# Where the sums of w_down for block 1 are made: in the second pass of block 0's second matrix, or in block 1's first matrix

## The chip, the core and the metric

The kernel runs on one core of a Trainium2 chip. The metric is the device time of one execution in microseconds; before the change it is 2035.29 us, the median of three runs (2033.35 to 2038.95). One execution was recorded by the hardware profiler. TensorE (PE) multiplies matrices, VectorE (DVE), ScalarE (ACT) and GpSimd (POOL) work on elements, SyncE (SP) issues DMA transfers. Each engine, and each queue of DMA issues, works in the order in which its instructions were written.

## The reference, cut to what matters

One layer: an S5 mixer with a gated linear unit, and behind it a gated feed-forward layer with a causal convolution of width 3, for 2048 frames, `D_MODEL` = 1024, `D_FF` = 2816. The change touches the feed-forward layer alone:

```python
def conv_ffn(xn, w_up, conv_w, conv_b, w_down):
    h = causal_dwconv(xn @ w_up, conv_w, conv_b)
    a, b = jnp.split(h, 2, axis=-1)
    return (jax.nn.silu(a) * b) @ w_down
```

`w_up` is 1024 x 5632 and `w_down` 2816 x 1024, in float32. The result is added to the residual.

## The kernel before

**Tiling.** The frames are taken in two blocks, `kb` = 0 and 1, of 1024 frames each. For each block the first matrix (`up`) multiplies by `w_up`, the convolution and the gate follow (`conv`), and the second matrix (`down`) multiplies by `w_down`. Float32 is kept by splitting each operand into a high and a low half in float16: one product is three matmuls of 128x512 (`mm3`, L76 to L78).

**First matrix.** It is done in 22 steps m, each by seven products in place of eight (a scheme of the Strassen kind over a 2x2 split). A product takes one weight chunk, a "unit" `("u", kb, m, i)`, and twelve matmuls into a PSUM bank `p`, of which six are in rotation. DVE and ACT take the banks out into `hu` (L1216 to L1230); the taps of the convolution (L1131, L1132) and the gate (L1135, L1137) follow some products later by a small calendar (`later`, `tick`).

**Second matrix.** Block 0 does it plainly, in two passes r = 0 and 1 over half of its frames each. A pass runs over 22 chunks f of 128 rows of `w_down`, two units `("p", 0, r, f, n)` each, with all eight PSUM banks `pq` in use, and starts on f = 0 and 1 together. Block 1 does it by seven products in four stages (`STAGES`), units `("d", 1, s, j, i)`. Five of the seven need sums or differences of rows j and j + 11 of `w_down`. With 11 values of j these are 55 sums; they are made ahead of time as units `("x", ...)` that no matmul uses, and are kept in DRAM.

**Weights.** `units` (L802 to L816) is the list of all units in the order in which they are fetched. `w_unit` (L876) takes the next of them, into the next of nine slots of a ring of `wc` tiles:

- If the chunk was made before, SyncE loads it from the DRAM tile `wcd`, 256 KB (L885).
- If not, it is made from float32 rows `fst` that SyncE has loaded, 512 KB each (L858, L861; four buffers). For a sum GpSimd first adds or subtracts (L907), into `xtmp` (one buffer) or in place. ACT then writes the high half (L908).
- At the next call of `w_units`, `w_flush` has DVE make the low half (L914), SyncE stores the chunk to `wcd` (L915), and rows used up are replaced by loads of the next ones.

`w_units` is called before each product with the index of that product's unit plus a lead: `LU` = 6 in the first matrix, `LD` = 5 in the second. The lead counts units, so those that no matmul uses count among them. At the end of each pass of block 0 the results are added to the residual tiles `res` (L1292) and stored; the 16 stores are issued by ACT (L1288). SyncE loads the residual (L1283).

Before the change the 55 sums stand in the second pass (r = 1) of block 0's second matrix, five per two f. Its own 44 units were made in the first pass and are read back from `wcd`. In block 1's first matrix all 154 units are read back from `wcd`.

Of the kernel before, what the change touches and what calls it, by code (L numbers as in the profile page):

```python
# [22 lines left out]
NF = 22  # L23
# [21 lines left out]
def tile_kernel(ctx: ExitStack, tc: tile.TileContext, x, meta, norm_mix, norm_ffn, w_in, lam_re, lam_im, log_dt,  # L45
# [95 lines left out]
    with ExitStack() as c2:  # L141
# [627 lines left out]
        p = NCB - 1  # L769
# [32 lines left out]
    units, loads, users = [], [], {}  # L802
    for kb_ in range(2):
        ms_ = range(2 * NP)
        seq_ = [(0, 1), (0, 2), (1, 1), (1, 2), (0, 4), (0, 7), (0, 5), (0, 6), (0, 3)] if kb_ == 0 else []
        for m in ms_:
            seq_ += [(m, i) for i in (1, 2, 6, 7, 4, 5, 3) if (m, i) not in seq_]
        units += [("u", kb_, m, i) for m, i in seq_]
        if kb_ == 0:
            sums = [("x", 0, s, j, i) for j in range(NH) for s, i in ((1, 0), (2, 0), (0, 0), (2, 1), (3, 0))]  # L810
            for r in range(2):
                for f in range(NF):
                    units += [("p", 0, r, f, 1), ("p", 0, r, f, 0)]
                    units += sums[len(sums) * f // NF:len(sums) * (f + 1) // NF] if r else []
        else:
            units += [("d", 1, s, j, i) for s, n in ((0, 2), (1, 2), (2, 2), (3, 1)) for j in range(NH) for i in range(n)]  # L816

# [636 lines left out]
```

## Time and profile before

| what | value |
|---|---|
| median of three runs | 2035.29 us |
| the profiled execution, its own time | 2040.73 us |
| its span, first to last instruction | 2038.9 us |
| mean granted TensorE clock | 0.979 |
| block 0, first matrix | about 758 to 1182 us of the span |
| block 0, second matrix, pass 0 / pass 1 | 1182 to 1301 / 1301 to 1430 us |
| block 1, first matrix / second matrix | 1430 to 1829 / 1829 to 2039 us |
| DMA moved | 329.92 MB, mean 162 GB/s |

How to read the rows that follow: a row of waits gives engine and line, what released it, the idle time in us in total, how often, and the longest. A row of the timeline gives start, duration, engine and line, what is written from what, and in brackets the idle time ahead of it with its releaser; a matmul's duration is longer than the step to the next one, since matmuls overlap. SPq and ACTq are the queues in which SyncE and ACT issue DMAs. Rows of the DMA view end in the median time from issue to landing. Rows of one line or tile give the durations in ns as min/median/max, or busy us and mean ns, then idle time and releasers.

### The profile page before, as it was taken

How to read it: one execution, taken by the hardware profiler on the slowest of the kernel's cores; microseconds unless marked ns; L12 is line 12 of the kernel's file. 1: busy time of each engine (PE TensorE's matmuls, PEld its weight loads, DVE VectorE, ACT ScalarE, POOL GpSimd, SP SyncE). 2: the span in 40 equal slices, each digit the busy share in tenths (PEclk: the TensorE clock that was granted, in tenths of full speed). 3: DMA queues.
4: the chain of work that ended last, by engine and by line, in shares of the span. 5: the costliest groups of instructions: out<-in, count | busy, mean ns of one | idle time of the engine just before them, and what ended most of it. 6: DMA issues, size and time to landing. Idle time of an engine off the chain costs nothing.

```text
span 2038.9 us, 28973 instructions
## 1 busy us (share of the span) xinstructions
PE 1923.3 (94%) x10992; PEld 957.5 (47%) x10992; DVE 1384.9 (68%) x1709; ACT 645.2 (32%) x1057; POOL 577.2 (28%) x644
## 2 busy tenths in 40 slices
PE   3699999689999999999999989999999999999999
PEld 3456666445444444444444434334444444444444
DVE  3489999944444348999999961345466666668982
ACT  5433423312222224544445441222222232322110
POOL 4221212400000014555555500366000001117630
PEclk9799999789999999999999999999999999999999
DMA  9967766958566656444444489999533333336443
GB/s 187 188 136 140 176 138 150 229 139 185 130 140 158 147 150 178 143 156 148 146 157 148 151 243 274 310 324 303 171 104 101 102 104 101 101 99 156 144 124 93
DMA packets 337223, 329.92 MB, mean 162 GB/s; under 512 B 150700, under 2 KB 238332, under 8 KB 337084
## 3 DMA queue, kind: packets, MB, share of 16 engines
q1 hardware_dynamic: 319164, 286.01, 52.9%
q0 software_dynamic: 8496, 27.30, 4.7%
q10 hardware_dynamic: 9424, 14.76, 2.9%
q8 instruction: 86, 1.41, 0.3%
q14 instruction: 53, 0.43, 0.1%
HBM read 183.82 MB, written 108.45 MB: 143 GB/s over the span
## 4 chain that ended last, share of the span: by engine, by line
PE 66%; DVE 8%; DMA 4%; issue 2%; ACT 1%; POOL 1%; SPq 1%; DVEq 0%; ACTq 0%; POOLq 0%
PE g L137 15%; PE p L78 11%; PE p L76 11%; PE p L77 11%; PE pq L76 3%; PE pq L77 3%; PE pq L78 3%; PE po L76 2%; PE po L77 2%; PE po L78 2%; DMA wc<-wcd 1%; DMA wcd<-wc 1%; DVE wc L914 1%; DVE y L1132 1%; DVE y L1131 1%
## 5 line engine op out<-in xcount | busy, mean ns | idle before, releaser
L76 PE MATMUL p<-hc,wc 128*128 128x512 f16 x1232 | 467.3, 379 | 2.3 <-DMA hc<-hl 1.7
L78 PE MATMUL p<-hc,wc 128*128 128x512 f16 x1232 | 467.5, 379 | 1.7 <-DVE wc L914 1.7
L77 PE MATMUL p<-hc,wc 128*128 128x512 f16 x1232 | 467.4, 379 | 0.9 <-DMA hc<-hl 0.9
L137 PE MATMUL g<-wg,yT 128*128 128x512 f16 x1536 | 334.3, 381 | 0.7 <-DMA yT<-yh 0.7
L914 DVE SCALAR_TENSOR_TENSOR wc<-fst,wc 128x512 f16<-128x512 f32 x209 | 184.7, 892 | 109.9 <-ACT wc L908 91.4
L137 PEld LDWEIGHTS <-yT 128*128 128x128 f16 x1536 | 150.2, 98 | 183.1 <-issue 2.6
L908 ACT ACTIVATE wc<-fst 128x512 f16<-128x512 f32 x209 | 125.9, 625 | 229.6 <-POOL fst L873 97.5
L78 PEld LDWEIGHTS <-wc 128*128 128x128 f16 x1232 | 120.2, 98 | 148.7 <-DVE wc L914 3.8
L76 PEld LDWEIGHTS <-wc 128*128 128x128 f16 x1232 | 120.1, 98 | 140.0 <-issue 1.8
L77 PEld LDWEIGHTS <-wc 128*128 128x128 f16 x1232 | 120.2, 98 | 138.9 <-DMA hc<-hl 1.2
L76 PE MATMUL pq<-wc,act 128*128 128x512 f16 x352 | 135.2, 384 | 16.6 <-DMA wc<-wcd 11.1
L76 PE MATMUL u<-hnT,win 128*128 128x512 f16 (+2 forms) x352 | 115.2, 337 | 25.6 <-DMA hnT<-hl 14.8
L77 PE MATMUL pq<-wc,act 128*128 128x512 f16 x352 | 135.1, 384 | 0.0
L78 PE MATMUL pq<-wc,act 128*128 128x512 f16 x352 | 134.8, 383 | 0.0
L77 PE MATMUL u<-hnT,win 128*128 128x512 f16 (+2 forms) x352 | 114.9, 337 | 16.9 <-DMA hnT<-hl 16.9
L76 PE MATMUL po<-wc,act 128*128 128x512 f16 x308 | 117.6, 382 | 3.4 <-DVE res L1292 3.4
L77 PE MATMUL po<-wc,act 128*128 128x512 f16 x308 | 117.6, 382 | 0.0
L78 PE MATMUL po<-wc,act 128*128 128x512 f16 x308 | 117.4, 381 | 0.0
L78 PE MATMUL u<-hnT,win 128*128 128x512 f16 (+2 forms) x352 | 115.0, 337 | 0.0
L1123 ACT ACTIVATE act<-hu,cwt 128x1024 f32<-128x1024 f32 x44 | 54.6, 1241 | 185.6 <-DVE hu L1224 141.3
L77 PEld LDWEIGHTS <-act 128*128 128x128 f16 x660 | 64.8, 98 | 99.1 <-issue 23.3
L1123 ACT ACTIVATE y<-hu,cwt 128x1024 f32<-128x1024 f32 x44 | 54.6, 1240 | 162.3 <-DVE hu L1224 123.2
(328 smaller groups left out, 2983.6 us busy)
## 6 DMA issues: line engine op xcount, KB each, us to landing
wc<-wcd SPq DMA_DIRECT2D x275, 256.0 KB, 2.7
wcd<-wc SPq DMA_DIRECT2D x253, 256.0 KB, 3.2
fst<-in_ffn_w_up_dram SPq DMA_DIRECT2D x44, 512.0 KB, 5.1
fst<-in_ffn_w_down_dram SPq DMA_DIRECT2D x44, 512.0 KB, 5.8
ud<-us SPq DMA_DIRECT2D x32, 258.0 KB, 5.3
U<-ud SPq DMA_DIRECT2D x16, 516.0 KB, 3.5
Toep<-kd SPq DMA_DIRECT2D x64, 128.0 KB, 5.4
yd<-yf POOLq DMA_DIRECT2D x8, 1024.0 KB, 7.6
```

What stands on the lines that cost most here:

```text
L76: PE.matmul(out=ps, lhsT=sh, rhs=mh, start=first, stop=False)
L77: PE.matmul(out=ps, lhsT=sh, rhs=ml, start=False, stop=False)
L78: PE.matmul(out=ps, lhsT=sl, rhs=mh, start=False, stop=last)
L137: PE.matmul(out=gps[t][o], lhsT=yT[t][:, a, dk], rhs=wg[b][:, dk, 512 * o:512 * o + 512], start=(dk == 0 and a + b == 0), stop=(dk == DK - ...
L908: A.activation(w[:, 0], src, AF.Copy, scale=GS)
L914: V.scalar_tensor_tensor(w[:, 1], src, GS, w[:, 0], op0=ALU.mult, op1=ALU.subtract)
L1123: A.activation(y, hu[:, 2:18], AF.Identity, bias=cwt[:, 3, c:c + 1], scale=cwt[:, 2, c:c + 1])
L1131: V.scalar_tensor_tensor(y, hu[:, 1:17], cwt[:, 1, c:c + 1], y, op0=ALU.mult, op1=ALU.add)
L1132: V.scalar_tensor_tensor(y, hu[:, 0:16], cwt[:, 0, c:c + 1], y, op0=ALU.mult, op1=ALU.add)
```

## The change

The 55 sums are taken out of the second pass and put between the units of block 1's first matrix: none in the first nine products, then two per five products, until the 143rd product of 154. Nothing else is edited; the number of instructions for the sums stays the same. All lines behind the edit have a number that is lower by one in the changed file (L915 is L914 there).

```diff
-        units += [("u", kb_, m, i) for m, i in seq_]
+        sums = [("x", 1, s, j, i) for j in range(NH) for s, i in ((1, 0), (2, 0), (0, 0), (2, 1), (3, 0))] * kb_
+        for n_, (m, i) in enumerate(seq_):
+            units.append(("u", kb_, m, i))
+            units += sums[max(0, n_ - 6) * 2 // 5:max(0, n_ - 5) * 2 // 5]
         if kb_ == 0:
-            sums = [("x", 0, s, j, i) for j in range(NH) for s, i in ((1, 0), (2, 0), (0, 0), (2, 1), (3, 0))]
-            for r in range(2):
-                for f in range(NF):
-                    units += [("p", 0, r, f, 1), ("p", 0, r, f, 0)]
-                    units += sums[len(sums) * f // NF:len(sums) * (f + 1) // NF] if r else []
+            units += [("p", 0, r, f, n_) for r in range(2) for f in range(NF) for n_ in (1, 0)]
```

**First place: SyncE's queue at the start of the second pass.** `wc<-wcd` loads a chunk of the pass (`wc_11611` is that of f = 0, `wc_11817` that of f = 3), `wcd<-wc` stores a chunk that was made. Before:

```order
L885 DMA wc_11611<-wcd 128x1024
L915 DMA wcd<-wc_11609 128x1024
L861 DMA fst_11639<-in_ffn_w_down_dram 128x1024
L885 DMA wc_11641<-wcd 128x1024
L915 DMA wcd<-wc_11643 128x1024
L885 DMA wc_11652<-wcd 128x1024
L915 DMA wcd<-wc_11649 128x1024
L885 DMA wc_11720<-wcd 128x1024
L915 DMA wcd<-wc_11722 128x1024
L885 DMA wc_11750<-wcd 128x1024
L885 DMA wc_11752<-wcd 128x1024
L915 DMA wcd<-wc_11744 128x1024
```

The same place in the changed kernel:

```order
L884 DMA wc_11611<-wcd 128x1024
L914 DMA wcd<-wc_11609 128x1024
L860 DMA fst_11639<-in_ffn_w_down_dram 128x1024
L884 DMA wc_11641<-wcd 128x1024
L884 DMA wc_11643<-wcd 128x1024
L884 DMA wc_11645<-wcd 128x1024
L884 DMA wc_11647<-wcd 128x1024
L884 DMA wc_11713<-wcd 128x1024
L884 DMA wc_11715<-wcd 128x1024
```

The stores of sums (all `wcd<-wc` behind the first) have left the queue, and loads of chunks follow each other.

**Second place: block 1's first matrix, early in its step m = 2.** SyncE's queue before is an unbroken row of chunk loads; in the changed kernel it reads:

```order
L914 DMA wcd<-wc_12653 128x1024
L860 DMA fst_12680<-in_ffn_w_down_dram 128x1024
L860 DMA fst_12682<-in_ffn_w_down_dram 128x1024
L884 DMA wc_12684<-wcd 128x1024
L884 DMA wc_12700<-wcd 128x1024
L914 DMA wcd<-wc_12702 128x1024
L884 DMA wc_12727<-wcd 128x1024
L884 DMA wc_12743<-wcd 128x1024
L884 DMA wc_12763<-wcd 128x1024
L914 DMA wcd<-wc_12765 128x1024
```

After each sum's store come two or three chunk loads; after the last sum of each j two loads of rows stand between. On DVE at the same place, before (`hu_2_1<-p_2_6` takes out the product i = 6 of m = 2, the rows on `y_1_1` are the taps and the gate of m = 1):

```order
L1220 TENSOR_TENSOR hu_2_1_12982<-p_2_6_13008,hu_2_1_12982 128x512
L1131 SCALAR_TENSOR_TENSOR y_1_1_12963<-hu_1_1_12853,cwt,y_1_1_12963 128x1024
L1132 SCALAR_TENSOR_TENSOR y_1_1_12963<-hu_1_1_12853,cwt,y_1_1_12963 128x1024
L1135 SCALAR_TENSOR_TENSOR y_1_1_12963<-act,y_1_1_12963 128x512
L1135 SCALAR_TENSOR_TENSOR act<-act,y_1_1_12963 128x512
L1222 TENSOR_TENSOR hu_2_1_12982<-p_2_7_13029,hu_2_1_12982 128x512
```

and in the changed kernel:

```order
L1219 TENSOR_TENSOR hu_2_1_12670<-p_2_6_12706,hu_2_1_12670 128x512
L1130 SCALAR_TENSOR_TENSOR y_1_1_12648<-hu_1_1_12527,cwt,y_1_1_12648 128x1024
L1131 SCALAR_TENSOR_TENSOR y_1_1_12648<-hu_1_1_12527,cwt,y_1_1_12648 128x1024
L1134 SCALAR_TENSOR_TENSOR y_1_1_12648<-act,y_1_1_12648 128x512
L1134 SCALAR_TENSOR_TENSOR act<-act,y_1_1_12648 128x512
L913 SCALAR_TENSOR_TENSOR wc_12702<-xtmp_1_12703,wc_12702 128x512
L1221 TENSOR_TENSOR hu_2_1_12670<-p_2_7_12729,hu_2_1_12670 128x512
```

The low half of a sum, L913, now stands between the gate's products and the next eviction. Its chunk `wc_12702` is stored by SyncE's row above, ahead of the load of `wc_12727`, which is the weight of the first product of m = 3.

## The prediction

> **What bounds the kernel now.** I read the page first, then the busy times by stage, then what TensorE waits for in each stage, then the order of time at those waits. The stages below are, in turn: the seven-product first matrix of block 0, pass r=0 and pass r=1 of block 0's second matrix, the first matrix of block 1, the second matrix of block 1.
>
> ```profile
> PE 1923.3 (94%) x10992; PEld 957.5 (47%) x10992; DVE 1384.9 (68%) x1709; ACT 645.2 (32%) x1057; POOL 577.2 (28%) x644
> ```
>
> ```profile
> core 0: us, PE busy (x) PEld busy (x) DVE busy (x) ACT busy (x) POOL busy (x), PEclk, DMA share, GB/s
> 758.00:1182.00 424.00, 418.24 (x2556) 197.95 (x2555) 401.98 (x439) 203.15 (x352) 230.16 (x239) 1.00 0.48 156
> 1182.00:1306.00 124.00, 120.02 (x550) 53.90 (x549) 46.01 (x65) 30.87 (x51) 11.36 (x12) 0.99 1.00 281
> 1306.00:1431.00 125.00, 113.79 (x513) 50.37 (x512) 59.19 (x59) 31.81 (x51) 70.83 (x52) 0.97 0.93 309
> 1431.00:1829.50 398.50, 397.95 (x1845) 179.97 (x1844) 249.21 (x298) 112.87 (x160) 35.50 (x59) 1.00 0.38 109
> ```
>
> TensorE is the bound: 94% of the span. In block 1's first matrix (fourth row) it has no hole at all: 398.5 us for 1845 recorded matmuls is 0.216 us from start to start, and this is the pace that I use below. That stage can only lose. The second pass (third row) is the only one of the four in which TensorE is visibly idle, with DMA at 309 GB/s. The waits of TensorE, for the second pass and then for block 1's first matrix:
>
> ```profile
> PE pq L76 <- DMA wc<-wcd: 11.1, 6, 5.1
> ```
>
> ```profile
> PE p L76 <- DMA wc<-wcd: 0.5, 1, 0.5
> ```
>
> Six waits, 11.1 us, all for a weight chunk that SyncE reads back from `wcd`. In order of time on TensorE, the first matmul of the pass, the longest wait with the slow stretch behind it, the next wait, the last matmul, and the one wait at the start of block 1:
>
> ```profile
> 1301.30 0.38 PE L76 MATMUL pq<-wc,act 128*128 128x512 f16 x1
> ...
> 1322.13 0.58 PE L76 MATMUL pq<-wc,act 128*128 128x512 f16 x1 [5.08 <-DMA wc<-wcd]
> 1322.52 0.63 PE L77 MATMUL pq<-wc,act 128*128 128x512 f16 x1
> ...
> 1326.77 0.38 PE L78 MATMUL pq<-wc,act 128*128 128x512 f16 x1
> ...
> 1352.50 0.38 PE L76 MATMUL pq<-wc,act 128*128 128x512 f16 x1 [1.76 <-DMA wc<-wcd]
> ...
> 1429.70 0.38 PE L78 MATMUL pq<-wc,act 128*128 128x512 f16 x1
> ...
> 1433.21 0.39 PE L76 MATMUL p<-hc,wc 128*128 128x512 f16 x1 [0.55 <-DMA wc<-wcd]
> ```
>
> After the 5.08 us wait the matmuls start 0.42 us apart until 1326.77, eleven steps at half speed (the mean granted clock of the pass, 0.97, has this in it): 2.3 us more that belong to that wait. After the 1.76 us wait there is no such stretch.
>
> Why the chunk was late shows on the other engines, ACT, then DVE, then SyncE's queue:
>
> ```profile
> 1300.99 11.63 ACTq L1288 DMA_DIRECT2D out_dram<-res  x16
> 1312.72 1.15 ACT L908 ACTIVATE wc<-fst 128x512 f16<-128x512 f32 x2 [11.18 <-DMA out_dram<-res]
> ```
>
> ```profile
> 1313.38 1.29 DVE L914 SCALAR_TENSOR_TENSOR wc<-fst,wc 128x512 f16<-128x512 f32 x2 [10.58 <-ACT wc L908]
> ```
>
> ```profile
> 1314.10 0.92 SPq L915 DMA_DIRECT2D wcd<-wc  x2
> 1315.12 0.91 SPq L861 DMA_DIRECT2D fst<-in_ffn_w_down_dram  x2
> 1316.08 0.90 SPq L885 DMA_DIRECT2D wc<-wcd  x2
> ```
>
> ACT issues the 16 output stores of pass 0; the high half of a sum (L908) stands behind them until 1312.72, its low half on DVE (L914) behind that, its store (L915) behind that, and in SyncE's queue the chunk stands behind the store: issued at 1316.08, there at 1322.1, while TensorE is idle for it from 1317.05 (1322.13 - 5.08).
>
> **The change part by part.**
>
> Removed from the second pass: 55 sums, each one GpSimd add, one ACT copy, one DVE subtraction and a 256 KB store, and 18 loads of `w_down` rows. SyncE's queue there is then 44 chunk loads and 8 loads of `res`, none of which waits for a sum (first place of the order above); and 5 units ahead are 2.5 steps of the loop over f, not 1.1, since the 55 sums no longer count among the 99 units of the pass. The DMA rows of the second pass, then of block 1's first matrix:
>
> ```profile
> wcd<-wc SPq DMA_DIRECT2D x51, 256.0 KB, 4.5
> wc<-wcd SPq DMA_DIRECT2D x44, 256.0 KB, 4.5
> fst<-in_ffn_w_down_dram SPq DMA_DIRECT2D x18, 512.0 KB, 6.1
> ```
>
> ```profile
> wc<-wcd SPq DMA_DIRECT2D x159, 256.0 KB, 2.6
> ```
>
> 309 GB/s x 125 us = 38.6 MB; 51 stores (13.4 MB) and 18 loads (9.4 MB) go, so some 16 MB in 114 us stay, 139 GB/s. Block 1's first matrix reads the same kind of chunk at 109 GB/s, lands it in 2.6 us and never waits. So I take all excess of the pass as gone: from 1301.30 to 1429.70 are 128.4 us for 527 steps, 527 x 0.216 = 113.8, **14.6 us**. The nearest bound the other way: only the wait whose cause is shown goes, 5.1 + 2.3 = 7.4 us. The 0.55 us wait at the start of block 1 goes too, since the last sums no longer fill the ring there: 0.6 us. What comes late next in the pass is nothing that I can name: SyncE then waits only for slots that TensorE left four units earlier.
>
> Added to block 1's first matrix, two sums per five products. The durations of one (GpSimd, DVE, ACT), and what SyncE waited for in this stage before:
>
> ```profile
> L907 POOL TENSOR_TENSOR xtmp<-fst,fst x22: 1261/1304/1792, 1293.6 to 1414.4; 128x512 f32<-128x512 f32 x22
> L907 POOL TENSOR_TENSOR fst<-fst x22: 1262/1592/1719, 1294.9 to 1417.5; 128x512 f32<-128x512 f32 x22
> L914 DVE SCALAR_TENSOR_TENSOR wc<-wtmp,wc x22: 679/683/687, 775.5 to 1172.2; 128x512 f16<-128x512 f32 x22
> L914 DVE SCALAR_TENSOR_TENSOR wc<-xtmp,wc x22: 680/930/1526, 1295.5 to 1423.0; 128x512 f16<-128x512 f32 x22
> L908 ACT ACTIVATE wc<-xtmp 128x512 f16<-128x512 f32 x20 | 12.6, 629 | 54.8 <-DMA wcd<-wc 37.6 <-POOL xtmp L907 17.2
> ```
>
> ```profile
> SPq L885 <- PE p L78: 326.6, 150, 2.3
> ```
>
> By throughput they are hidden: GpSimd 55 x 1.45 = 80 us onto 35.5; DVE 55 x 0.93 = 51 onto 249; ACT 55 x 0.63 = 35 onto 113; all far below 398.5. Block 0's first matrix kept TensorE fed with DVE at 402 of 424 us. DMA grows to (43.4 + 14.4 + 9.4) MB in 400 us = 168 GB/s, near block 0's 156.
>
> What counts is order. Before, SyncE waited for TensorE alone, so chunks came as early as the ring allows. Now each sum's store waits for DVE, and the chunk loads queue behind it: counted out in the order, the first load behind a store is needed four products after the product whose weights were being asked for, 4 x 12 x 0.216 = 10.4 us. The worst place is the second one shown in the order, where the subtraction stands behind a burst of taps. In the trace of before that burst is:
>
> ```profile
> 1583.64 0.69 DVE L1220 TENSOR_TENSOR hu<-p,hu 128x512 f32<-128x512 f32 x1 [1.83 <-PE p L78]
> ...
> 1588.09 0.69 DVE L1222 TENSOR_TENSOR hu<-p,hu 128x512 f32<-128x512 f32 x1
> ```
>
> The eviction starts when its product ends (1583.6), the burst ends at 1588.1: 4.5 us. Add the subtraction 0.7, the store's place in the queue 0.46 (0.92 for two, above) and a landing of 2.6: 8.3 of 10.4 us, no wait. Behind the last of each five sums stand two loads of 512 KB as well, 0.9 us of queue, and a chunk that shares the DMA with them lands in 4.5 to 6.1: 11.1 to 12.7, late by 0.7 to 2.3. There are eleven such places, but only about four of them fall behind a burst; the others have 2 to 4 us less ahead of them. Bounds: nothing (a dense stage cannot gain) and 4 x 2.3 = 9 us; I take **2 us**, nearer to nothing, as most places have slack. Such waits are shorter than 3 us, so I add no slow stretch.
>
> GpSimd's halo copies (L1208) now stand behind sums, and ACT's high halves ahead of silu and copies; both stand some products ahead of their readers, and TensorE has six banks, 15 us, before an eviction holds it. These I cost at nothing; that cover gone, they would show as waits for `hu`.
>
> Sum: 14.6 + 0.6 - 2 = **13.2 us** less. The profiled run took 2040.73 us (span 2038.9), so 2027.5 under the profile; it is 5.4 above the median of the runs, 2035.29, and I carry the difference over: **2022.1 us**.
>
> The subtractions on DVE took 0.683 us where GpSimd made no sums beside them and 0.930, up to 1.526, where it did. The Trainium skill, page "SBUF — State Buffer", section "Who interferes with whom", has the rule: a DVE instruction with two inputs in SBUF contends with a GpSimd instruction that reads SBUF, and whichever starts later is blocked. The trace agrees in sign. It speaks against this change, which moves the sums to where DVE's taps run; by it alone 55 x 0.85 us, 47 us, would be added to DVE's work, an estimate, and what that would do is the third rival.
>
> **The rivals.**
>
> *The second pass keeps its other waits.* Only the first wait has its chain shown; the other five could come from `res` and chunk loads themselves. For it: DMA at 93%. Against it: the pass before ran at 100% DMA without a wait for weights. Then 7.4 + 0.6 - 2 = 6 us: 2029.3.
>
> *The waits move along.* Most of the eleven places cost what the worst of them cost, 11 x 0.9 = 10 us: gain 5.2, 2030.1.
>
> *Slower: DVE's lag outgrows the four products.* Blocked by GpSimd, two operations of a burst take 0.85 us more each (1.526 - 0.68), and chunks land in 6.1 instead of 2.6: 5.2 us on top of 8.3 is 3.1 beyond the 10.4 at the worst places, and about 1 us at the middling ones. The point is 15.2 / 55 = 0.28 us per sum: above it the change loses. Half the places at 1.2 us give 27 x 1.2 = 32, a loss of 17: 2052. For it: DVE's 930 ns median. Against it: DVE has 149 us idle in the stage, in holes of 1.3 to 1.9 us after most evictions, which eat such lags.
>
> That the sums stay where they were is ruled out by the order.
>
> **How the numbers follow.** Forecast 0.72, the pass keeping waits 0.09, waits moving along 0.12, slower 0.07. A measurement of this kernel can tell about 0.3%, 6.1 us, from no change: below 2029.2 is faster. The forecast is (2017 to 2027); the two middle cases lie astride 2029.2, about half each. Faster 0.72 + 0.11 = 0.83, the same 0.10, slower 0.07. Range: low end the full 15.2 us and half the spread of the three runs (2.8) below it, 2017; high end the two middle cases with 2 us more, 2032; the slower case stays outside.
>
> **What would show it.** Right: no wait of `pq` for `wcd` after 1301, the pass 114 us long, chunk landings there below 3 us; block 1's first matrix within 399 to 402 us. Wrong in the first term: waits at f=3 or later that still name `wcd`. Wrong in the second: many waits of `p` for `wc<-wcd` in block 1, with SyncE's L915 waiting for DVE's L914 ahead of them, and L914 well above 0.9 us. What would make it wrong altogether: loads held by something that I took for free, above all SyncE standing at a sum's store whose GpSimd add waits behind halo copies.

## The result, and the profile after

The changed kernel takes 2020.88 us (median of four runs, 2020.46 to 2024.19) beside 2035.04 us of the kernel before (2033.35 to 2038.95): a ratio of 0.9928, with a 95% interval of 0.9903 to 0.9954. Run again later, beside other runs of the kernel before, it gave 0.9912 [0.9887, 0.9936]. It is faster by 14.2 us, or 0.7%, and the interval lies wholly below 1; 13.2 us were forecast. Its profiled run took 2021.29 us, span 2019.4.

The busy times of the changed kernel by stage; the columns are those of the table in the prediction, the rows are the second pass, block 1's first matrix and block 1's second matrix:

```profile
1293.40:1407.30 113.90, 113.90 (x530) 51.66 (x528) 5.53 (x8) 0.00 (x0) 3.11 (x6) 1.00 0.56 155
1407.30:1809.90 402.60, 399.41 (x1850) 180.59 (x1849) 302.98 (x353) 142.44 (x214) 115.27 (x112) 1.00 0.49 163
1809.90:2019.40 209.50, 201.53 (x926) 90.72 (x923) 150.41 (x163) 30.60 (x50) 91.68 (x65) 0.99 0.46 127
```

The second pass has no hole: TensorE is busy for all of its 113.9 us, at the full granted clock, and DMA has fallen from 309 to 155 GB/s. Block 1's first matrix has gained DVE, ACT and GpSimd work and some holes: 402.6 us. The last stage is as it was.

In order of time on TensorE: first and last matmul of the pass, first matmul of block 1, its three waits, and the first matmul of the last stage.

```profile
1293.46 0.38 PE L76 MATMUL pq<-wc,act 128*128 128x512 f16 x1
...
1407.20 0.38 PE L78 MATMUL pq<-wc,act 128*128 128x512 f16 x1
1407.42 0.38 PE L76 MATMUL p<-hc,wc 128*128 128x512 f16 x1
...
1553.35 0.39 PE L76 MATMUL p<-hc,wc 128*128 128x512 f16 x1 [0.73 <-DVE hu L1229]
...
1683.20 0.39 PE L76 MATMUL p<-hc,wc 128*128 128x512 f16 x1 [0.17 <-DMA wc<-wcd]
...
1719.33 0.39 PE L76 MATMUL p<-hc,wc 128*128 128x512 f16 x1 [2.29 <-DMA wc<-wcd]
...
1809.99 0.38 PE L76 MATMUL po<-wc,act 128*128 128x512 f16 x1
```

The pass takes 1407.20 - 1293.46 = 113.74 us between its first and last start, in place of 128.40, and block 1 follows one step later. From the pass's first matmul to that of the last stage are 516.5 us, before 528.2 (1829.5 - 1301.3): 11.7 us less. The profiled spans differ by 19.5 us; the other 7.8 us lie ahead of the pass, which starts at 1293.5 and not at 1301.3.

How the largest wait comes about shows on DVE, SyncE's queue and TensorE:

```profile
1707.33 1.47 DVE L1130 SCALAR_TENSOR_TENSOR y<-hu,cwt,y 128x1024 f32<-128x1024 f32 x1
1708.83 1.28 DVE L1131 SCALAR_TENSOR_TENSOR y<-hu,cwt,y 128x1024 f32<-128x1024 f32 x1
1710.15 1.23 DVE L1136 SCALAR_TENSOR_TENSOR y<-act,y 128x1024 f32<-128x1024 f32 x1
1711.29 0.68 DVE L913 SCALAR_TENSOR_TENSOR wc<-fst,wc 128x512 f16<-128x512 f32 x1
```

```profile
1712.00 0.32 SPq L914 DMA_DIRECT2D wcd<-wc  x1
1712.41 1.55 SPq L860 DMA_DIRECT2D fst<-in_ffn_w_down_dram  x2
1714.06 0.86 SPq L884 DMA_DIRECT2D wc<-wcd  x2
```

The low half L913 stands behind a burst of taps and gate, SyncE's store behind L913, two row loads behind the store, and then comes the chunk that TensorE starts to wait for at 1717.04 (1719.33 - 2.29): issued at 1714.06 and landed 5.2 us later, while the row loads were under way.

### The profile page after: what moved, and what is told of

Read it like the earlier page. It is cut to its first block, busy times and chain, and to the rows that moved or that the text cites. A ratio compares the mean times of both kernels' runs of the same rounds, so it can differ in the third digit from the quotient of the medians.

```text
span 2019.4 us, 28924 instructions
## 1 busy us (share of the span) xinstructions
PE 1914.0 (95%) x10992; PEld 954.7 (47%) x10992; DVE 1381.8 (68%) x1709; ACT 641.9 (32%) x1057; POOL 584.1 (29%) x644
## 4 chain that ended last, share of the span: by engine, by line
PE 69%; DVE 7%; DMA 2%; issue 2%; POOL 1%; ACT 1%; SPq 0%; DVEq 0%; ACTq 0%; POOLq 0%
PE g L137 15%; PE p L76 11%; PE p L78 11%; PE p L77 11%; PE pq L76 4%; PE pq L78 4%; PE pq L77 4%; PE po L76 2%; PE po L77 2%; PE po L78 2%; DVE y L1131 1%; DVE y L1130 1%; DMA fst<-in_ffn_w_up_dram 1%; DVE S L552 1%; DVE S L550 1%
## 5 line engine op out<-in xcount | busy, mean ns | idle before, releaser
L913 DVE SCALAR_TENSOR_TENSOR wc<-fst,wc 128x512 f16<-128x512 f32 x209 | 179.6, 868 | 93.3 <-ACT wc L907 86.5
L1207 POOL COPY hu<-halo 128x2 f32<-128x2 f32 x44 | 15.3, 361 | 331.2 <-DMA out_dram<-res 224.2
```

The source lines that it names most:

```text
L913: V.scalar_tensor_tensor(w[:, 1], src, GS, w[:, 0], op0=ALU.mult, op1=ALU.subtract)
L1207: PO.tensor_copy(hus[m, e][:, 0:2, 0], halo[:, 2 * n + NF * ab + e])
```

## The experiments

A table of all of them, in us, from each run's own profile: the second pass from its first to its last matmul (113.7 without a hole), block 1's first matrix from its first matmul to that of the next stage (398.9 without a hole), and the single time or, where there are several, the median. The kernel before, run beside them, took 2032.4 to 2036.8 us, so a single time in the last column tells little, and the lengths of the stages tell more.

| kernel | second pass | block 1, first matrix | time |
|---|---|---|---|
| before | 128.4 | 399.6 | 2035.04 |
| changed | 113.7 | 402.6 | 2020.88 |
| e1, sums from f = 4 | 145.0 | 398.9 | 2047.52 |
| e2, 88 free stores, ACT | 119.3 | 401.5 | 2030.62 |
| e3, 88 free stores, SyncE | 114.0 | 402.5 | 2023.00 |
| e4, empty units | 113.7 | 403.0 | 2025.43 |
| e5, changed once more | 113.7 | 403.2 | 2020.11 |
| e6, row loads last | 113.7 | 398.9 | 2016.52 |
| e7, before, sums' DMAs by ACT | 121.6 | 398.9 | 2027.22 |
| e8, changed, sums' DMAs by ACT | 114.9 | 398.9 | 2016.93 |
| e10, before, lead 7 | 131.0 | 400.0 | 2038.30 |
| e11, e7 with lead 7 | 124.2 | 399.7 | 2030.74 |
| e12, empty units and 88 stores | 126.1 | 405.0 | 2031.76 |
| e13, the same, slots for chunks alone | 113.7 | 401.6 | 2020.02 |

**The first wait and ACT's output stores (e1).** The kernel before, with the sums kept from the first four steps:

```diff
-units += sums[len(sums) * f // NF:len(sums) * (f + 1) // NF] if r else []
+units += sums[len(sums) * max(0, f - 4) // (NF - 4):len(sums) * max(0, f - 3) // (NF - 4)] if r else []
```

> The kernel before, its 55 sums still in the second pass but spread over f = 4 to 21, so that none stands behind the 16 output stores that ACT issues at the start of the pass. If those stores held the first chunk (theory): the wait at f = 3 (5.1 us, with 2.3 us at half speed behind it) is gone, and the pass takes 121 to 123 us in place of 128.4; the short waits of 0.6 to 1.8 us stay or grow a little, since there are now three sums per f. If the first wait comes from DMA load at the end of the pass before (rival): a wait of 4 us or more stays at f = 2 to 4.

The wait at f = 3 is gone; the first one of the pass comes 37 us into it. But the pass grew to 145.0 us: with three sums per step of f in place of two and a half, the later waits grew to nine, of 0.4 to 4.7 us. The theory holds for the first wait and fails for the size of the rest. That the number of units per step sets the rest is only suggested here, since a step also holds more sums to make and store.

**Bytes alone (e2, e3).** The changed kernel with stores of `hc` to a spare tensor in each step of the second pass, issued by ACT (e2) or by SyncE (e3):

```diff
+if r:
+    for k in range(4):
+        A.dma_start(out=spare[4 * f + k], in_=hc[0][:, 0:2])    # e3: SY
```

> The changed kernel with the bytes of the sums put back into the second pass as 88 stores of 256 KB, four per f, issued by ACT and tied to nothing. If the waits came from order and dependencies (theory): TensorE waits less than 1 us in the pass in total, which takes 114 to 115 us at 300 GB/s or more. If they came from the load on the DMA engines (rival): 5 us or more of waits for chunks, the pass at 119 us or more.

> The same 88 stores, but issued by SyncE, in the queue of the chunk loads. They wait for no sum, only for a place among the transfers in flight. If the dependency of the stores on the sums is what held the queue (theory): 0 to 2 us of waits in the pass. If a store ahead of the loads in the same queue is enough (rival): 5 us or more.

From SyncE's queue (e3) the pass moves 354 GB/s, more than the kernel before, a chunk lands in 5.1 us (three landings recorded), and TensorE hardly waits: 114.0 us. So neither the bytes nor a store ahead of a load in the queue are enough. From ACT's queue (e2) the same stores cost 5.6 us: the pass is as long as the rival had it, with 3.5 us of waits and a stretch at half speed behind the longest. What SyncE waits for there:

```profile
SPq L885 <- DMA spare<-hc: 38.6, 20, 5.4
```

SyncE's chunk loads wait for ACT's stores to land (in e3 for 4.3 us in all). In e2's trace the transfers of both queues share eight semaphores, and in 95 of 96 cases the landing that an issue of SyncE or ACT waited for was that of the transfer which had used the same semaphore before. So e2 is no clean test of the load on the DMA engines; it shows that in this program a second queue's transfers hold the first, since at most about eight are under way for both together.

**A short lead, and slots taken, without the load (e4).** The changed kernel with 55 units in the second pass that do nothing but count in the lead and take a slot number each:

```diff
-units += [("p", 0, r, f, n_) for r in range(2) for f in range(NF) for n_ in (1, 0)]
+        units += [("p", 0, r, f, 1), ("p", 0, r, f, 0)]
+        units += [("e", 0, k) for k in range(55 * f // NF, 55 * (f + 1) // NF)] if r else []
...
+if units[n][0] == "e":
+    return
```

> The changed kernel with 55 empty units in the second pass: they count in the lead of five and take a slot number of the ring, and do nothing. The lead is then 1.1 steps of f, about 5.7 us, in place of 2.5. Theory: the short lead alone costs little where a chunk lands in 2.6 us and nothing holds the queue: 0 to 1 us of waits, the pass at 114 to 115 us. Rival, the lead is the cause: the five short waits come back, 4 to 7 us, the pass at 118 to 121 us.

113.7 us and no wait: without further load on the queue, neither the short lead nor the lost slots cost anything.

**The queue (e7), and a longer lead (e10, e11).** The kernel before, with the sums' stores and their rows' loads, all but the first four, taken out of SyncE's queue:

```diff
-SY.dma_start(out=wcd[kept[key(u)]], in_=w)
+(A if u[0] == "x" else SY).dma_start(out=wcd[kept[key(u)]], in_=w)
...
-SY.dma_start(out=t, in_=w_down[0, l[1] * P:(l[1] + 1) * P])
+(A if l[0] == "x" and pos["load"] > 69 else SY).dma_start(out=t, in_=w_down[0, l[1] * P:(l[1] + 1) * P])
```

> The kernel before, its sums in the second pass, but the stores of the sums and the loads of their rows are issued by ACT, so that SyncE's queue in the pass has chunk loads alone. Theory (stores that wait for DVE hold the chunk loads behind them in SyncE's queue): the waits fall from 14.6 us of excess to 4 or less, the pass at 114 to 118 us. Rival (sums and chunks share nine ring slots, and a slot is not free until a sum's store has landed): the waits stay, 120 us or more, with SyncE's chunk loads waiting for transfers of wcd.

121.6 us: 6.8 of the 14.6 us of excess go, 7.9 stay, between the two. What goes is the first wait: with its stretch at half speed it made 7.5 us, and in e7 the first wait makes 1.1. The later waits come to 7.1 us before and 6.7 in e7. The longest of them, 3.5 us, has a holder of its own: SyncE stands 4.5 us before a load of `res` until an earlier load of `res` has landed, and only then issues the chunk. As in e2, ACT's transfers share the semaphores, so e7 takes one holder out of SyncE's queue and brings another in. The other two kernels have a lead of 7 units in the second pass (`LD + 2 * r`), e11 together with the edit of e7.

> The kernel before with a lead of 7 units in place of 5 in the second pass, 1.6 steps of f or 8 us in place of 1.1 and 5.7. If short lead and loaded DMA together make the five later waits (theory): they shrink to 2 us in total or less, the first wait behind ACT's output stores stays, the pass at 120 to 123 us. If the stores that wait for DVE are enough by themselves (rival): 126 us or more.

> Both remedies in the kernel before, sums still in the second pass: stores of the sums and loads of their rows issued by ACT, and a lead of 7 units. Theory: nothing holds SyncE's queue and a chunk that lands in 6 us has 8, the pass at 114 to 116 us, the whole gain of the change without moving a sum. Rival (the sums' use of the nine slots or DMA at 93% holds chunks whatever the lead): 119 us or more.

Both missed: 131.0 and 124.2 us, each 2.6 us above the same kernel with a lead of 5 (one profile each). A longer lead does not bring the chunks earlier. A unit fetched seven ahead wants the slot of the unit two behind, and SyncE and ACT stand before that slot: in e10 ACT's high halves waited 45.0 us for stores of sums to land, 37.6 before.

**Both harmless loads together, and the slots (e12, e13).** e12 joins the edits of e4 and e3. In e13 the empty units take no slot number:

```diff
-sl_ = n % NR
+sl_ = pos["slot"] % NR
+pos["slot"] += 1
```

> The changed kernel with both harmless loads of the second pass together: the 55 empty units that shorten the lead to 5.7 us, and the 88 stores of 256 KB in SyncE's queue, on which a chunk lands in 5.1 us. Theory (each alone 0, together late): 3 to 8 us of excess, the pass at 117 to 122 us. Rival (only a store that waits for a sum holds chunks): 115 us or less.

> As the kernel with empty units and 88 stores, but the empty units take no slot number: the nine slots serve chunks alone, while the lead of five units still counts the empty ones. If the short lead is what makes chunks late under load (theory): the pass stays at 122 us or more. If it is the slots, which each chunk then had to take two steps of f after their last use (rival, favoured by the two kernels with a lead of seven, in which nothing was gained): 116 us or less.

e12: 126.1 us, an excess of 12.3 without any sum in the pass, more than expected. e13, the same stores and the same short lead: 113.7 us, no wait at all, at 345 GB/s. What SyncE's chunk loads wait for from TensorE in the pass, e12 and then e13 (the second view reaches 5 us into block 1):

```profile
SPq L892 <- PE pq L79: 32.9, 17, 4.4
```

```profile
SPq L893 <- PE pq L79: 12.9, 12, 4.1
```

This settles it for the changed kernel under these loads, since only the slots differ. A unit takes the slot of the unit nine before it. With 4.5 units per step of f that is the same chunk of the step two before, and TensorE leaves it 36 matmuls, 36 x 0.216 = 7.8 us, before it needs the new one. Under load the chunk stands behind other transfers in SyncE's queue and then took 5.0 to 7.1 us to land (three of e12's four waits): it comes late. With 2 units per step the slot is free four steps, 20.7 us, before the need, and SyncE has run ahead. The fourth and longest wait of e12, 4.3 us, shows the slots at their tightest: steps 20 and 21 run together, so the first chunk of f = 21 is needed at their fourth matmul, 15 matmuls or 3.2 us after its slot came free.

The trace of the kernel before has the same pattern. Five of its six late chunks were issued 2.8 to 6.8 us after TensorE had left their slot and landed 5.5 to 7.6 us after that; the sixth is the first chunk of f = 21. No run freed the slots in that kernel itself.

**Block 1's first matrix (e5, e6, e8).** e5 is the changed kernel unaltered. e6 issues the two row loads behind the chunk loads of the same call, up to the next sum:

```diff
 for l in [l for l in wst if users[l] == u]:
     del wst[l]
-    w_load()
+    owed.append(l)
...
 def w_units(upto):
     w_flush()
     while pos["unit"] <= upto:
         ...
+        if owed and key(units[pos["unit"]]) not in made:
+            w_pay()
         w_unit()
+    w_pay()
```

> The changed kernel once more, unaltered, beside the kernels that follow. Pass 113.7 us, block 1's first matrix 402 to 403 us with the same two or three waits for chunks that stand behind row loads (products 56 and 119, counted from 0); what comes ahead of the feed-forward layer differs by some us from execution to execution.

> The changed kernel with one order turned round: the two loads of w_down rows that replace a used pair are issued behind the chunk loads of the same call, not ahead of them. Theory (a chunk that is late queues 0.9 to 1.6 us behind these loads and shares the DMA engines with them): the 2.3 us wait at product 119 and the 0.7 us wait at product 56 shrink to less than 0.5 us each, block 1's first matrix 399.5 to 400.5 us in place of 402.6. Rival (the burst on DVE alone makes them late): waits of 1 us or more stay, 401.5 us or more. The median time falls by 0 to 3 us, less than rounds can tell.

e5 has one wait, where two or three were expected, at product 119 again (2.4 us, with a stretch at half speed behind it), and 403.2 us. In e6 the stage has no hole, 398.9 us. The same place in SyncE's queue, now with the awaited chunk ahead of the row loads:

```profile
1709.07 0.32 SPq L914 DMA_DIRECT2D wcd<-wc  x1
1709.48 0.85 SPq L884 DMA_DIRECT2D wc<-wcd  x1
1710.42 0.86 SPq L860 DMA_DIRECT2D fst<-in_ffn_w_down_dram  x2
1711.33 0.42 SPq L884 DMA_DIRECT2D wc<-wcd  x1
```

e8 is the changed kernel with the edit of e7.

> The changed kernel with the stores of the sums and the loads of their rows issued by ACT. Theory: SyncE waits for TensorE alone again in block 1's first matrix, no wait for chunks is left, 399.3 to 400 us. Against it: ACT, standing at a store that waits for DVE, takes product i = 1 and the convolution late; then TensorE waits for banks, or DVE for ACT, and the stage stays at 402 us or grows.

Block 1's first matrix is without a hole here too, 398.9 us; the pass before it has one wait of 1.0 us. Against the kernel before, e6 is at 0.9901 [0.9881, 0.9921], 2016.52 us, and e8 at 0.9906 [0.9885, 0.9927], 2016.93, in the same rounds as e5 with 2020.11. Both stand below the changed kernel by 3 to 4 us, as their stage does, but the intervals of the ratios overlap. e6 is the version I would keep.

## Why the prediction was right, point by point

- **The second pass.** All its excess was forecast to go, 14.6 us, and 128.40 - 113.74 = 14.66 went. The rival in which the other five waits stay, at 7.4 us, fell.
- **Why it goes.** For the first wait the account holds: ACT's output stores made it (e1 lost it), and the sums' stores in SyncE's queue passed it on to the chunk (e7: 6.8 us). For the later waits, the other half, the prediction gave less load on DMA and a longer lead. Less load holds: at the changed kernel's load a chunk is never late, even with a short lead and few slots (e4). The lead was named wrongly. "5 units ahead are 2.5 steps of the loop over f, not 1.1" is a lead in the order of the program, and a short one costs nothing where slots are free (e13). What the sums took was slots: nine slots are two steps of f with them and four and a half without, which under load was worth 12.3 us (e12 against e13). The parts don't add up, since each is harmless alone.
- **The start of block 1.** The 0.55 us wait there is gone, as forecast.
- **Block 1's first matrix.** Forecast were 2 us of holes, within 0 to 9; there are 402.57 - 398.85 = 3.7, and 4.3 in e5, so the stage ends just outside the 399 to 402 us that the prediction gave as a sign of being right. (Its other sign, chunk landings below 3 us in the second pass, stays open: the trace has no landing there.) The place was right: the two largest stand at products 56 and 119, whose chunks queue behind the last store of five sums, the row loads and a burst of taps, both among the places behind a burst. The profile names an eviction for the first of them, but it is that of the product just before, whose bank product 56 does not use; the semaphore of the chunk's load was complete at 1553.31, 0.04 us before TensorE went on. SyncE's queue has that chunk behind two row loads, and in e6 the wait is gone with the others. The assumption that such a wait is too short for a stretch at half speed failed in e5.
- **Throughput.** DVE was forecast at 249 + 51 = 300 us and came to 303; GpSimd at 116 and came to 115; ACT at 148 and came to 142; DMA at 168 GB/s and came to 163.
- **The slower rival** did not come. DVE's work rose by 302.98 - 249.90 = 53.1 us; 55 low halves at the undisturbed 0.683 us are 37.6, so about 15.5 us are what GpSimd's work beside it cost DVE. The trace bears this out: of the low halves of sums and of the gate's products (L1148), those that overlap no GpSimd addition take at most 0.693 us, those that overlap one up to 1.76, and the 61 overlapped evictions, which read one operand from PSUM, at most 0.693. The rule of the Trainium skill, page "SBUF — State Buffer", section "Who interferes with whom", agrees with this trace in sign; the 47 us estimated by it did not come, since 38 of the 55 low halves overlap no addition.
- **The total.** 15.4 us gained and 3.7 lost are 11.7; the medians differ by 14.2. The other 2.5 us aren't explained by the three stages. Ahead of them the profiled runs of kernels that are equal up to there differ by up to 11.8 us (second matrix of block 0 from 1169.9 to 1181.7), and the profile of before was the latest. So the sum was near the measured time partly by luck, and a single pair of spans (19.5 us apart) would have told too much.

## What to carry to other kernels

When work that nothing waits for shares a ring of buffers and an issue queue with transfers that the bounding engine waits for, count the slots: units per step times the steps that a transfer needs, its time in the queue included, must be below the number of slots, and a longer lead in the program cannot stand in for a free slot. Move such work to a stage in which the ring turns slowly, and there put the awaited transfer ahead of the large ones that nobody awaits. Judge the result stage by stage, from first to last instruction, as the part of the program that didn't change can differ by more than the change brings.

## What the runs showed of the hardware that was not expected

- Transfers of one queue can hold those of another: SyncE's chunk loads waited 38.6 us for stores that ACT had issued (e2), and 4.3 us when SyncE had issued the same ones (e3). The hold is in the semaphores of this program; that the chip's queues hold each other is not shown.
- How long an idle time must be for the half-speed stretch is not fixed. In e10 a wait of 2.97 us was followed by it and one of 2.98 us was not:

```profile
1327.72 0.59 PE L76 MATMUL pq<-wc,act 128*128 128x512 f16 x1 [2.97 <-DMA wc<-wcd]
1328.10 0.63 PE L77 MATMUL pq<-wc,act 128*128 128x512 f16 x1
...
1366.19 0.38 PE L76 MATMUL pq<-wc,act 128*128 128x512 f16 x1 [2.98 <-DMA wc<-wcd]
1366.41 0.38 PE L77 MATMUL pq<-wc,act 128*128 128x512 f16 x1
```

- GpSimd's sums slow DVE by how their times fall: the low half of a sum in `xtmp` had a median of 930 ns in the second pass, where 15 of 22 overlapped a GpSimd addition, and of 684 ns in block 1's first matrix, where 3 of 22 did:

```profile
L913 DVE SCALAR_TENSOR_TENSOR wc<-xtmp,wc x22: 681/684/1753, 1418.6 to 1763.3; 128x512 f16<-128x512 f32 x22
```
